# Letting the last 256 tokens enter a phase's first two GEMM tiles unnormed, in a hybrid attention and Mamba-2 backbone

## The chip, the cores and the metric

The kernel runs on one core of a Trainium2 chip. The metric is the device time of one execution in microseconds, the median of several runs. The engines are named as in the profile: PE is TensorE (PEld is its weight load), DVE VectorE, ACT ScalarE, POOL GpSimd, SP the engine that issues the DMAs.

## The reference, cut to what matters

Two layers over 512 latent tokens and a prefix of 256 context tokens, with 1024 features. Layer 0 mixes tokens with grouped-query attention, layer 1 with a bidirectional Mamba-2 state-space mixer (SSD), and a gated convolutional FFN of width 2816 follows each. Every sub-layer starts with an RMS norm and a modulation by a shift and a scale:

```python
def rms_norm(x, g):
    xf = x.astype(jnp.float32)
    y = xf * lax.rsqrt(jnp.mean(xf * xf, axis=-1, keepdims=True) + EPS)
    return (y * g.astype(jnp.float32)).astype(x.dtype)

def modulate(x, shift, scale):
    return x * (1 + scale) + shift
...
```

So the input of a sub-layer's first GEMM is, for feature d and token t, x[d, t] · gain[d] · rs[t] + shift[d], with gain = g · (1 + scale) and rs[t] the reciprocal root of the token's mean square. A GEMM with weights W gives for token t the product rs[t] · (W (x · gain)) + W shift: the factor rs and the term W shift can be put in behind the product.

## The kernel before, in words

Features lie on the 128 partitions and tokens in the free dimension, so the 1024 features are eight row tiles (KT = 8, index m where they are made, k where they are read). Every GEMM of width 1024 is done in three matmuls for one weight block and one row tile (`mm3`, L105, L106, L108): both factors are split into a high and a low half of a shorter format (`wh`, `wl`; `hh`, `hl`), and the products high·high, high·low and low·high are summed in PSUM. `load_w` (L85, L87) makes the two halves of a weight block: ScalarE casts the high one, VectorE subtracts for the low one.

A phase ends with `down` (attention output, FFN down product) or with the SSD's output product. They add their products to the residual rows `X`, one row tile m after the other, with a VectorE instruction per tile (L897 in `down`). They go over the tokens in segments (`ending`): first the 256 context tokens, then latent tokens 0 to 255, then latent tokens 256 to 511. As the rows of a segment are added, ScalarE squares them and they are summed (`Norm.sq`, L356 to L363; GpSimd adds most of them). When all eight are in, `rstd_rows` makes rs: two small matmuls over the partitions (`ss`, L267), a few small steps on VectorE and ScalarE (`rsa`, `rsy`, `rsu`, `rb`, L270 to L278), a transposition on TensorE (`rsT`, L284), and a copy by ScalarE (`rs`, L376). Then `modulated` makes each of the eight input rows of the segment: VectorE multiplies x · gain · rs (`ht`, L312). In even rows ScalarE adds the shift and writes the high half (L321), and VectorE makes the low half (L322); in odd rows ScalarE adds the shift (L317), casts the high half (L318), and GpSimd makes the low half (L319).

`first_tiles` holds the first two GEMM tiles of the next phase (`ps_first`, two PSUM tiles of 1024 columns, tag S). Their products run first for the segments that have their norm already and at the end for the last 256 latent tokens, while the norm of those goes on in the generator `bg`. There are three such boundaries. The first is from the attention's output product to FFN 0 (first products from 413 us on), the second from FFN 0 to the SSD (from 974 us on), the third from the SSD's output product to FFN 1 (from 1534 us on; no context tokens there). At the second, the two first tiles are `ps_dt`, the step sizes of the state space, and the first x tile. ScalarE reads `ps_dt` (`dte`, `dt`, L1031 and L1032), a chain of VectorE instructions follows (`dtu`, L1035 on, a reciprocal, four scans), and with its sums `acs` TensorE transposes (`ps_dtT`, L1252) and makes `ps_end` (L1258) from a VectorE copy of them (`acsT`, L1253). The convolution of x and B (`xf`, `Bf`, L1077) shares VectorE with that chain; `ps_xt` (L1121) and `ps_bt` (L1128) transpose x and B.

Each engine works through its own queue in a fixed order. A scheduler sets that order when the kernel is built, from the order of the program and from estimates of how long things take, so moving code also moves instructions on other engines.

## Time and profile before

| what | value |
|---|---|
| runs | 1911.81, 1906.7, 1911.2 us; median 1911.2 |
| the profiled execution, its time | 1909.82 us |
| the profiled execution, its span | 1908.0 us |
| granted TensorE clock, mean | 0.995 |
| busy share PE, DVE, ACT, POOL | 98%, 69%, 44%, 14% |
| chain that ended last: PE, DVE, issue, ACT | 79%, 9%, 4%, 2% |

The profile is of one execution. Its span runs from the first to the last instruction; the 1.8 us more of its time lie around it. A row of the timeline has start, duration, engine, line, operation, output and input, and the idle time before it with what released it. Matmuls overlap: one of 256 columns is listed with 0.28 us, while the next starts 0.12 us after it.

### The profile page before, as it was taken

What the parts mean: (1) busy time and instruction counts of PE and PEld (TensorE: products, weight loads), DVE (VectorE), ACT (ScalarE), POOL (GpSimd) and SP (SyncE); (2) the same over time, 40 slices, a digit from 0 to 9 for tenths busy, and PEclk for the clock granted to TensorE, in tenths of its full rate; (3) what the DMA queues carried; (4) which work ended last, traced back from release to release, by engine and by line L of the source; (5) the groups of instructions that cost most, each with busy time, mean ns of one, the idle gap of its engine ahead of it and who ended that gap; (6) DMA issues with size and microseconds to landing.
All of it is one profiled execution on the core that took longest, in us unless ns stands there. A gap on an engine that the chain in (4) does not pass through costs nothing.

```text
span 1908.0 us, 27239 instructions
## 1 busy us (share of the span) xinstructions
PE 1864.2 (98%) x10696; PEld 1527.1 (80%) x10696; DVE 1321.9 (69%) x1953; ACT 844.5 (44%) x1446; POOL 263.8 (14%) x246
## 2 busy tenths in 40 slices
PE   8899999989999999999989999999999999999999
PEld 6674546588888888888888888888888878888887
DVE  5578989678777777544488867777788466565555
ACT  3645644354122222222266677776666352323331
POOL 2200000031000000000040344344334210000000
PEclk8999999999999999999999999999999999999999
DMA  9123341014433555222223434434443223323232
GB/s 338 56 71 106 111 150 55 7 56 167 136 124 121 174 187 175 67 67 67 66 79 103 116 108 122 122 111 133 122 143 111 89 78 90 99 88 111 88 100 89
DMA packets 73424, 210.00 MB, mean 110 GB/s; under 512 B 8912, under 2 KB 14416, under 8 KB 73168
## 3 DMA queue, kind: packets, MB, share of 16 engines
q1 hardware_dynamic: 73296, 208.26, 35.0%
q8 instruction: 84, 1.38, 0.3%
q14 instruction: 44, 0.36, 0.1%
HBM read 198.79 MB, written 6.82 MB: 108 GB/s over the span
## 4 chain that ended last, share of the span: by engine, by line
PE 79%; DVE 9%; issue 4%; ACT 2%; POOL 1%; DMA 1%; SPq 0%; DVEq 0%; POOLq 0%; ACTq 0%
PE ps_up L106 10%; PE ps_up L108 10%; PE ps_up L105 10%; PE ps_d L105 6%; PE ps_d L108 6%; PE ps_d L106 6%; PE ps_in L108 4%; PE ps_in L106 4%; PE ps_in L105 4%; PE ps_o L687 2%; PE ps_s L723 2%; PE ps_st L1147 2%; DVE ht L312 1%; PE ps_wo L108 1%; PE ps_wo L105 1%
## 5 line engine op out<-in xcount | busy, mean ns | idle before, releaser
L87 DVE TENSOR_TENSOR wl<-wst,wh 128x1024 fp32r<-128x1024 f32 x209 | 260.4, 1246 | 243.3 <-PE ps_up L106 137.5
L85 ACT CAST wh<-wst 128x1024 fp32r<-128x1024 f32 x211 | 221.2, 1049 | 426.5 <-DMA wst<-in_wup 336.9
L106 PE MATMUL ps_up<-hlf,wh 128*128 128x512 f32 x1008 | 357.0, 354 | 0.0
L105 PE MATMUL ps_up<-hhf,wh 128*128 128x512 f32 x1008 | 356.9, 354 | 0.0
L108 PE MATMUL ps_up<-hhf,wl 128*128 128x512 f32 x1008 | 356.8, 354 | 0.0
L105 PEld LDWEIGHTS ps_up<-hhf,wh 128*128 128x128 f32 x1008 | 190.6, 189 | 26.5
L108 PEld LDWEIGHTS ps_up<-hhf,wl 128*128 128x128 f32 x1008 | 190.5, 189 | 26.4
L106 PEld LDWEIGHTS ps_up<-hlf,wh 128*128 128x128 f32 x1008 | 190.6, 189 | 26.2
L105 PE MATMUL ps_in<-hhs,wh 128*128 128x512 f32 (+1 forms) x560 | 204.4, 365 | 0.0
L106 PE MATMUL ps_in<-hls,wh 128*128 128x512 f32 (+1 forms) x560 | 199.4, 356 | 0.0
L108 PE MATMUL ps_in<-hhs,wl 128*128 128x512 f32 (+1 forms) x560 | 198.7, 355 | 0.0
L105 PE MATMUL ps_d<-hdh,wh 128*128 128x512 f32 (+1 forms) x568 | 193.6, 342 | 1.4 <-DVE X L897 1.2
L108 PE MATMUL ps_d<-hdh,wl 128*128 128x512 f32 (+1 forms) x568 | 193.5, 341 | 0.0
L106 PE MATMUL ps_d<-hdl,wh 128*128 128x512 f32 (+1 forms) x568 | 193.0, 340 | 0.3 <-DVE hdl L87 0.3
L897 DVE SCALAR_TENSOR_TENSOR X<-ps_d,mod,X 128x512 f32<-128x512 f32 (+1 forms) x224 | 124.9, 583 | 34.1 <-PE ps_d L108 33.6
L106 PEld LDWEIGHTS ps_d<-hdl,wh 128*128 128x128 f32 x568 | 106.6, 188 | 14.9 <-DVE hdl L87 0.7
L105 PEld LDWEIGHTS ps_d<-hdh,wh 128*128 128x128 f32 x568 | 106.3, 188 | 14.8 <-DVE X L897 1.4
L105 PEld LDWEIGHTS ps_in<-hhs,wh 128*128 128x128 f32 x560 | 105.9, 189 | 15.1 <-issue 1.0
L108 PEld LDWEIGHTS ps_in<-hhs,wl 128*128 128x128 f32 x560 | 105.8, 189 | 14.8
L108 PEld LDWEIGHTS ps_d<-hdh,wl 128*128 128x128 f32 x568 | 106.7, 188 | 13.1
L106 PEld LDWEIGHTS ps_in<-hls,wh 128*128 128x128 f32 x560 | 106.0, 189 | 13.2
L726 ACT ACTIVATE pr<-ps_s 128x1024 f32<-128x1024 f32 x56 | 57.1, 1020 | 97.5 <-PE ps_s L725 95.6
(341 smaller groups left out, 3493.7 us busy)
## 6 DMA issues: line engine op xcount, KB each, us to landing
wst<-in_wup SPq DMA_DIRECT2D x88, 512.0 KB, 3.6
wada<-in_adaT SPq DMA_DIRECT2D x56, 512.0 KB, 4.0
wst<-in_win SPq DMA_DIRECT2D x48, 512.0 KB, 3.7
wst<-in_wdown SPq DMA_DIRECT2D x44, 512.0 KB, 4.1
E<-ad SPq DMA_DIRECT2D x64, 256.0 KB, 6.8
wada<-in_adaB SPq DMA_DIRECT2D x24, 512.0 KB, 4.9
ec<-ead SPq DMA_DIRECT2D x64, 128.0 KB, 5.4
wst<-in_wout SPq DMA_DIRECT2D x16, 512.0 KB, 3.6
```

The source lines that it names most:

```text
L85: keep(nc.scalar.copy(hi, src))
L87: keep(eng.tensor_tensor(lo, src, _r(hi), ALU.subtract))
L105: mm(out, wh, ah, start=first, stop=False)
L106: mm(out, wh, al, start=False, stop=False)
L108: mm(out, wl, ah, start=False, stop=last)
L312: nc.vector.scalar_tensor_tensor(t[:, c0:c1], ap, g.moda[layer][ca][:, m, v : v + 1], rs[:, c0:c1], ALU.mult, ALU.mult)
L687: nc.tensor.matmul(po[S64[e], :n], v, pr[:, 512 * e + off : 512 * e + off + n], start=first, stop=last)
L723: nc.tensor.matmul(outs[e], a[S64[e], k], b[S64[e], q], start=i == 0, stop=False)
L726: nc.scalar.activation(pr, ps, AF.Exp)
L897: nc.vector.scalar_tensor_tensor(ap, o[:, c0:c1], gate[:, m, v : v + 1], ap, ALU.mult, ALU.add)
L1147: nc.tensor.matmul(ps[:, d * 256 : (d + 1) * 256], Bt[:, t * P : (t + 1) * P], xw[d][t], start=t == ts[0], stop=t == ts[-1])
```

## The change

The last segment (latent tokens 256 to 511, `LAST`) now enters the first two tiles as x · gain, without rs and without the shift. Each of its rows is made when it is added to `X` (`Norm.scaled`): ScalarE writes the high half (L373 of the new kernel), VectorE the low half (L374). The products of these rows come first, then those of the context, then those of latent tokens 0 to 255. The input of this last run has two more columns, which hold the shift (`Norm.bias`), so that W · shift falls out of the same matmuls in two PSUM columns. For them the input tiles got eight more floats in front: every input row now begins 32 bytes into its tile. Once rs of the last segment is there, three VectorE instructions per tile put it right in PSUM: a copy of two columns, the product with rs, the sum with W · shift (L472 to L474).

The rows that have their norm (`Norm.rows`) are made where `down` and `first_tiles` call for them: those of the context from the last `down` tiles on and between the products of the first run, those of tokens 0 to 255 between the products of the second, and those of the last segment, which the rest of the phase needs normed, in the third. All low halves of these rows are now VectorE's; GpSimd makes none of them. In the SSD the second x tile of the first group goes to two PSUM banks (`single`). At the third boundary the last tile of the output product is done in halves of its depth, alternating between the two column halves, and the weights of the first tiles are loaded ahead of it. The constant of ones is kept in the shorter format. The lines left out are the passing of the new objects from phase to phase.

```diff
+PAD = 8
+def wide(g, name):
+    return tuple(g.p.tile([P, PAD + L], F32R, tag=f"h{L}", bufs=16, name=f"{p}{name}") for p in ("hh", "hl"))
 def htiles(g, n, name):
+    if n == L:
+        return tuple(t[:, PAD:] for t in wide(g, name))
...
+    def scaled(self, x, m):
+        g, nc = self.g, self.g.nc
+        layer, ca, _ = self.a
+        t = self.tile(f"xa{self.name}")
+        hi, lo = t[:, : L // 2], t[:, L // 2 :]
+        gain = g.moda[layer][ca][:, m, 0:1]
+        (ap, _, _), = parts(x[0][m], *LAST[1:])
+        nc.scalar.activation(hi, ap, AF.Identity, scale=gain)
+        nc.vector.scalar_tensor_tensor(lo, ap, gain, _r(hi), ALU.mult, ALU.subtract)
+        self.early[m] = hi, lo
+    def bias(self, m):
+        g, nc = self.g, self.g.nc
+        layer, _, cb = self.a
+        b = g.mod[layer][cb][:, m, 0:1].broadcast_to([P, 2])
+        hi, lo = (t[:, PAD - 2 : PAD] for t in self.w[m])
+        nc.scalar.copy(hi, b)
+        nc.vector.tensor_tensor(lo, b, _r(hi), ALU.subtract)
...
         for m in range(KT):
-            modulated(g, self.h[i][m], x[i], rs, a, b, *self.a, self.streams[i][1], m, pool=m % 2)
+            if i == a == 0:
+                self.bias(m)
+            modulated(self.g, self.h[i][m], x[i], self.rs[seg], a, b, *self.a, self.streams[i][1], m)
             yield
...
-def first_tiles(g, ws, norm, bg):
-    ends = ending(norm.streams)
-    for _ in gemm_in(g, tiles, norm.h, (0, L), [ends[:-1], ends[-1:]]):
-        next(bg, None)
-    for _ in bg:
+def first_tiles(g, ws, norm, x):
+    nc = g.nc
+    half = L // 2
     tiles = [(S(g, "ps_first"), w) for w in ws]
+    chain = norm.chain(LAST)
+    runs = [(2 * half, lambda k: norm.early[k]), (half - 2, lambda k: tuple(t[:, PAD - 2 : PAD + half] for t in norm.w[k]))]
+    if len(norm.streams) > 1:
+        runs.insert(1, (3 * half, lambda k: norm.h[1][k]))
+    todo = norm.todo + [None]
+    for i, (c0, h) in enumerate(runs):
+        if i == len(runs) - 1:
+            for _ in chain:
+                pass
+            todo[i] = norm.rows(LAST, x)
+        n = 0
+        for ps, w in tiles:
+            for k in range(KT):
+                ks = slice(k * P, (k + 1) * P)
+                o = ps[:, c0 : c0 + h(k)[0].shape[-1]]
+                mm3(g, (w[0][:, ks], w[1][:, ks]), [(o, h(k))], k == 0, k == KT - 1)
+                next(chain, None)
+                if n % 2:
+                    next(todo[i], None)
+                n += 1
...
+    for ps, _ in tiles:
+        v, b = ps[:, 2 * half : 3 * half], g.p.tile([P, 2], F32, tag="rst", bufs=8, name="wb")
+        nc.vector.tensor_copy(b, ps[:, half - 2 : half])
+        nc.vector.tensor_tensor(v, v, norm.rs[LAST], ALU.mult)
+        nc.vector.tensor_scalar(v, v, b[:, 0:1], None, ALU.add)
...
@@ down
                 if norm:
                     norm.sq((i, a, b), x, m)
+                    if (i, a, b) == LAST:
+                        norm.scaled(x, m)
             next(bg, None)
+            if norm and gi == 1 and m > 4:
+                next(todo[0])
...
@@ ssd
-            ps = ps_x0 if gi == j == 0 else gemm(ld(j), (1, 0))
+            ps = (ps_x0[:, :L], ps_x0[:, L:T]) if gi == j == 0 else gemm(ld(j), (1, 0), gi == 0)
...
+    half = [Bank(g, "ps_wo")[:, : L // 2] for _ in SEGS[0]]
+    for ks in (range(8), range(8, 16)):
+        for (_, a, b), ps in zip(SEGS[0], half):
+            m_tile(m, ws, ps, a, b, ks, bg)
+            if ks[0]:
+                add_out(m, ps, a, b)
+                nxt.sq((0, a, b), [xn], m)
+                if a:
+                    nxt.scaled([xn], m)
+                else:
+                    bg = nxt.chain((0, a, b), 1)
...
```

The order of the instructions is best seen at three places. The first is TensorE's queue near the end of the attention's output product, where the first products of FFN 0 come in (`ps_d` is a tile of the output product, `hhol` and `hlol` the attention's result, `hhf_0` and `hlf_0` normed rows). Before:

```order
L267 MATMUL ssf_3975<-ones,sqf_3890 128x1 x2
L105 MATMUL ps_first<-hhf_0_3612,wh 128x256
L106 MATMUL ps_first<-hlf_0_3613,wh 128x256
L105 MATMUL ps_first<-hhf_0_3612,wh 128x256
L106 MATMUL ps_first<-hlf_0_3613,wh 128x256
L105 MATMUL ps_d_3988<-hhol_3220,wh 128x256
L106 MATMUL ps_d_3988<-hlol_3221,wh 128x256
```

And after (`xaf` is a scaled row):

```order
L108 MATMUL ps_d_3990<-hhol_3588,wl 128x256
L105 MATMUL ps_first<-xaf_3923,wh 128x256
L106 MATMUL ps_first<-xaf_3923,wh 128x256
L108 MATMUL ps_first<-xaf_3923,wl 128x256
L105 MATMUL ps_first<-xaf_3940,wh 128x256
L106 MATMUL ps_first<-xaf_3940,wh 128x256
L108 MATMUL ps_first<-xaf_3940,wl 128x256
L105 MATMUL ps_first<-xaf_3957,wh 128x256
L106 MATMUL ps_first<-xaf_3957,wh 128x256
L108 MATMUL ps_first<-xaf_3957,wl 128x256
L284 MATMUL rsTf_4008<-cst,rbf_3971 128x128 x2
L105 MATMUL ps_d_4012<-hhol_3220,wh 128x256
```

Four products of a normed row stood between the tiles of the output product before; now eleven products of scaled rows stand there (two of a second weight block, which repeat a row above, are in the queue as well), and all of the other scaled products follow the last `ps_d`.

The second place is VectorE's queue at the second boundary, from the last normed rows to the chain through `dtu` (`hls` low halves, `hhs` high halves, `rss` the norm's factor, `wb` the two columns of W · shift). Before:

```order
L322 SCALAR_TENSOR_TENSOR hls_4_4313<-ht,mod_92,hhs_4_4312 128x256
L87 TENSOR_TENSOR wl<-wst,wh 128x1024
L322 SCALAR_TENSOR_TENSOR hls_6_4317<-ht,mod_92,hhs_6_4316 128x256
L1063 MEMSET raw_9259 128x2 x3
L1063 MEMSET raw_9260 128x2
L1025 TENSOR_SCALAR na<-na 128x1
L1063 MEMSET raw_9260 128x2 x2
L1035 TENSOR_SCALAR dtu<-dte 128x384
```

And after:

```order
L332 SCALAR_TENSOR_TENSOR hls_5_4351<-ht,mod_94,hhs_5_4350 128x256
L322 SCALAR_TENSOR_TENSOR ht<-X,moda_102,rss 128x256 x2
L472 COPY wb<-ps_first 128x2 x2
L332 SCALAR_TENSOR_TENSOR hls_6_4353<-ht,mod_94,hhs_6_4352 128x256
L332 SCALAR_TENSOR_TENSOR hls_7_4355<-ht,mod_94,hhs_7_4354 128x256
L473 TENSOR_TENSOR ps_first<-ps_first,rss 128x256 x2
L474 TENSOR_SCALAR ps_first<-ps_first,wb 128x256 x2
L1109 TENSOR_SCALAR na<-na 128x1
L1147 MEMSET raw_9331 128x2 x3
L1147 MEMSET raw_9332 128x2 x3
L87 TENSOR_TENSOR wl<-wst,wh 128x1024
L1119 TENSOR_SCALAR dtu<-dte 128x384
```

The correction of the two tiles (L473, L474) now stands behind all rows of the last segment and ahead of `dtu`, and a weight split moved from the rows to a place just ahead of `dtu`.

The third place is TensorE's queue at the end of the C tile of the SSD's first group (`ps_in` with `hhs_7` is its last product, `ps_in` with `hhs_0` the first of the z tile). Before:

```order
L1252 MATMUL ps_dtT<-cst,dt 128x128 x3
L105 MATMUL ps_in<-hhs_0_4304,wh 128x512
L106 MATMUL ps_in<-hls_0_4305,wh 128x512
L108 MATMUL ps_in<-hhs_0_4304,wl 128x512
L105 MATMUL ps_in<-hhs_1_4306,wh 128x512
L106 MATMUL ps_in<-hls_1_4307,wh 128x512
L1258 MATMUL ps_end<-acsT,cst 128x192 x2
L1121 MATMUL ps_xt<-cst,xf 128x128 x8
L108 MATMUL ps_in<-hhs_1_4306,wl 128x512
L1121 MATMUL ps_xt<-cst,xf 128x128 x4
```

And after:

```order
L108 MATMUL ps_in<-hhs_7_4354,wl 128x512
L1336 MATMUL ps_dtT<-cst,acs 128x128 x3
L1336 MATMUL ps_dtT<-cst,dt 128x128 x3
L1342 MATMUL ps_end<-acsT,cst 128x192 x2
L1205 MATMUL ps_xt<-cst,xf 128x128 x12
L105 MATMUL ps_in<-hhs_0_4340,wh 128x512
L106 MATMUL ps_in<-hls_0_4341,wh 128x512
L108 MATMUL ps_in<-hhs_0_4340,wl 128x512
```

Five products of the z tile that stood ahead of `ps_end`, and a sixth that stood among the `ps_xt`, now stand behind all of them.

More of the change, by code (lines that the diff above doesn't have):

```diff
@@ L460, in attention @@
     for _ in range(24):
-        nc.tensor.matmul(warm[:, :P], g.ones, g.ones, start=True, stop=True)
+        nc.tensor.matmul(warm[:, :P], g.warm, g.warm, start=True, stop=True)
     acc = t3(g, "acc", n=L)
@@ L625, in q_units @@
             nc.scalar.copy(qs[:, c0 : c0 + n], ps[:, :n])
-    onesr = g.const.tile([P, P], F32R, name="onesr")
-    nc.scalar.copy(onesr, g.ones)
+    onesr = g.onesr
     id2 = g.const.tile([P, HD], F32, name="id2")
@@ L885, in down @@
     bg = iter(())
-    for group in order:
+    todo = []
+    for gi, group in enumerate(order):
         for m in ms:
@@ L904, in down @@
                 pass
-            bg = norm.gen(group[0], x, 2)
-    return bg
+            if group[0] != LAST:
+                bg = norm.chain(group[0])
+                todo.append(norm.rows(group[0], x))
+    if norm:
+        norm.todo = todo
 def ffn(g, layer, streams, x, h, first, nxt=None, side=iter(()), after=()):
@@ L989, in ffn, with ssd @@
         ln_exp(g)
-    return flush(pend, [[s] for s in ending(streams)], nxt, after), wf
-def ssd(g, x, norm, wf, bg, close):
+    flush(pend, [[s] for s in ending(streams)], nxt, after)
+    return wf
+def ssd(g, x, norm, wf, close):
     nc, I, tc = g.nc, g.I, g.tc
@@ L998, in ssd @@
     h = norm.h
-    ps_dt, ps_x0 = first_tiles(g, wf, norm, bg)
+    ps_dt, ps_x0 = first_tiles(g, wf, norm, x)
     ph = ExitStack()
@@ L1013, in ssd, with gemm @@
     tok = lambda t: slice(t * P + (2 if t >= 4 else 0), (t + 1) * P + (2 if t >= 4 else 0))
-    def gemm(w, streams):
+    def gemm(w, streams, single=False):
+        if single:
+            ps = [Bank(g, "ps_in1") for _ in range(2)]
+            for i in streams:
+                for _ in gemm_in(g, [(ps[i], w)], h, (0, 0), [[(i, 0, (L, C)[i])]]):
+                    pass
+            return ps[0], ps[1]
         ps = S(g, "ps_in")
@@ L1017, in gemm @@
             pass
-        return ps
+        return ps[:, :L], ps[:, L:T]
     H2 = 64
@@ L1417, in body @@
     wf = firsts(g, I["wup"][0, 0], I["wup"][0, NFT])
-    bg = down(g, ws, [g.oT[f] for f in (5, 6, 7)], g.mod[0][2], streams, x, [[s] for s in ending(streams)], nrm)
-    first = first_tiles(g, wf, nrm, bg)
+    down(g, ws, [g.oT[f] for f in (5, 6, 7)], g.mod[0][2], streams, x, [[s] for s in ending(streams)], nrm)
+    first = first_tiles(g, wf, nrm, x)
     pha.close()
```

78 lines of the change are left out of this document (45 added, 33 removed).

## The prediction

> **What bounds the kernel now.** The page comes first: TensorE is busy nearly all the time, so the end moves only where TensorE stands still or where it gets other work to do.
>
> ```profile
> span 1908.0 us, 27239 instructions
> PE 1864.2 (98%) x10696; PEld 1527.1 (80%) x10696; DVE 1321.9 (69%) x1953; ACT 844.5 (44%) x1446; POOL 263.8 (14%) x246
> ```
>
> TensorE's work is not changed by more than a few columns, so I read the three places the diff touches, first by equal windows (columns: length, then busy time and count of each engine, granted clock, DMA).
>
> ```profile
> 393.00:413.00 20.00, 19.42 (x157) 18.81 (x157) 15.76 (x34) 11.88 (x29) 10.08 (x12) 1.00 0.09 28
> 413.00:433.00 20.00, 16.57 (x128) 15.37 (x128) 17.37 (x37) 12.17 (x33) 9.13 (x11) 1.00 0.25 79
> 433.00:453.00 20.00, 18.74 (x126) 16.99 (x126) 14.51 (x23) 13.62 (x22) 4.21 (x4) 1.00 0.40 159
> 973.90:993.90 20.00, 16.41 (x127) 15.19 (x128) 17.39 (x37) 12.27 (x33) 9.12 (x11) 1.00 0.56 185
> 1525.00:1545.00 20.00, 17.36 (x119) 15.56 (x117) 13.71 (x31) 9.27 (x23) 3.79 (x4) 0.91 0.18 54
> ```
>
> In the 20 us ahead of the first boundary (attention to FFN) 0.6 us is idle, at it 3.4 and then 1.3. The second (FFN to SSD, 973.9) has the same shape. The third (SSD to FFN) loses 2.6 in its first 20 us, and only there the granted clock falls, to 0.91. VectorE is at 87% at the first two: it is the next engine to watch. The waits of TensorE between 404 and 446 say who was late:
>
> ```profile
> PE ps_first L106 <- POOL hlf L319: 1.5, 3, 0.7
> PE rsTf L284 <- DVE rbf L278: 1.2, 2, 1.0
> PE ps_d L105 <- DVE X L897: 1.1, 1, 1.1
> PE ps_first L105 <- ACT hhf L318: 0.5, 1, 0.5
> PE ps_first L106 <- DVE hlf L322: 0.5, 1, 0.5
> ```
>
> Nine stalls, 4.8 us (columns: total, times, longest). Behind a stall the next matmul starts 0.22 and not 0.12 us later (1537.05, 1537.27 below), so each loses 0.1 more: 5.7 us.
>
> At the third boundary the stalls are only part of it:
>
> ```profile
> 1533.87 0.50 PE L105 MATMUL ps_first<-hhf,wh 128*128 128x256 f32 x2 [0.64 <-ACT hhf L321]
> 1537.05 0.39 PE L106 MATMUL ps_first<-hlf,wh 128*128 128x256 f32 x1 [1.04 <-POOL hlf L319]
> 1537.27 0.31 PE L108 MATMUL ps_first<-hhf,wl 128*128 128x256 f32 x1
> 1538.45 0.41 PE L108 MATMUL ps_first<-hhf,wl 128*128 128x256 f32 x1
> 1538.66 0.41 PE L105 MATMUL ps_first<-hhf,wh 128*128 128x256 f32 x1
> 1553.94 0.28 PE L106 MATMUL ps_first<-hlf,wh 128*128 128x256 f32 x1
> 1554.06 0.28 PE L108 MATMUL ps_first<-hhf,wl 128*128 128x256 f32 x1
> ```
> ```profile
> 1534.00:1537.00 3.00, 1.61 (x8) 1.00 (x8) 3.00 (x6) 2.57 (x6) 1.46 (x2) 1.00 0.58 178
> 1537.00:1540.00 3.00, 2.95 (x15) 2.95 (x16) 3.00 (x8) 1.82 (x4) 0.87 (x1) 0.57 0.00 0
> 1540.00:1543.00 3.00, 3.00 (x24) 2.98 (x23) 1.84 (x6) 2.24 (x7) 1.26 (x2) 0.87 0.01 3
> ```
>
> The 96 first products last from 1533.87 to 1554.18, 20.3 us. At 0.12 each they need 11.5, with three early 512-column matmuls, a sum and a transpose 12.8: 7.5 us lost, and 0.64 ahead of them, 8.1. Inside it lie some 3 us at a granted clock of 0.57, where matmuls start 0.21 instead of 0.12 us apart: 14 matmuls by 0.09, 1.3 us. That stretch follows three microseconds in which TensorE was busy 1.61.
>
> The Trainium skill, TensorE: Matmul & The Clock Gate, Part 1, has the array at half rate after an idle window of about 3.4 us, until it has been busy as long. The trace agrees on the depth and the length; but here sparse work was enough, no wait was longer than 1.04 us. Dense products should end this stretch; I count it inside the 8.1.
>
> **The change part by part.** *First boundary.* When the last `down` tile ends, the 48 products of the unnormed last 256 tokens need only scaled rows, and most of those rows exist: 48 × 0.12 = 5.8 us of work wait for TensorE where before it had four products and then stalled on `X`, `rbf` and `hhf`. What may run late is VectorE. All low halves are now its own (12 move from GpSimd), and it makes 8 more for the scaled rows. Prices:
>
> ```profile
> 993.93 2.07 DVE L312 SCALAR_TENSOR_TENSOR ht<-X,moda,rss 128x256 f32<-128x256 f32 x5 [1.03 <-ACT rss L376]
> 981.77 1.04 DVE L312 SCALAR_TENSOR_TENSOR ht<-X,moda,rss 128x256 f32<-128x256 f32 x1
> L312 DVE SCALAR_TENSOR_TENSOR ht<-X,moda,rss 128x256 f32<-128x256 f32 x19 | 11.1, 618 | 2.0 <-ACT rss L376 2.0
> 986.32 0.42 DVE L361 TENSOR_TENSOR sqs<-sqs 128x256 f32<-128x256 f32 x1
> 983.13 1.21 DVE L87 TENSOR_TENSOR wl<-wst,wh 128x1024 fp32r<-128x1024 f32 x1
> 1034.03 0.29 DVE L1279 TENSOR_SCALAR nacs<-acsT 128x256 f32<-128x256 f32 x1
> ```
>
> Five 256-column steps back to back take 2.07, 0.40 each; a lone one took 1.04 while GpSimd made a low half beside it, and the mean of the nineteen `ht` at the second boundary is 0.62. With GpSimd gone from here I take 0.40 (bounds 0.40 and 0.62): its rows are the ones with nothing beside them. Behind the last `X` update stand 20 `ht` and 20 low halves, 16 us, and 3.8 of other things (one weight split 1.2, the statistics, squares, one scaled row), then the correction in PSUM (two by 0.42, two by 0.29, small copies: 1.6). Up to the last normed row that the first tiles read, the queue is 24 × 0.40 + 3.8 = 13.4 us; TensorE's own work over that stretch is 133 × 0.12 = 16.0. So it fits, by a little: I leave 1.0 us for stalls, where a low half waits for ScalarE's high half and the queue runs dry for a moment. The eight pairs of the last 256 tokens then run beside the next tile, at 0.80 a pair against three 512-column matmuls (0.23 each, below) or 0.69: another 0.9. The correction ends some 8 us after the products; FFN tile 0's convolution reads it, and TensorE has two more tiles before that is wanted. Gain 5.7 − 1.9 = **3.8** (0 if every step stays at 0.62, 5.7 if no stall is left). The two extra columns are 1/128 of 48 products, 0.05 us; the 16 two-column bias steps (8 on ScalarE, 8 on VectorE) and the earlier weight loads come while the last `down` or output tiles run, where both engines wait for TensorE. The 32-byte start I take at nothing; no row of before has a shifted read, so its price is a rival.
>
> *Second boundary.* At the end of the first tiles TensorE is 5.7 − 1.0 = 4.7 ahead. But here their reader is a chain:
>
> ```profile
> 1002.64 0.58 ACT L1031 ACTIVATE dte<-ps_first,par 64x384 f32<-64x384 f32 x1 [0.42 <-PE ps_first L108]
> 1005.32 0.36 DVE L1035 TENSOR_SCALAR dtu<-dte 128x384 f32<-128x384 f32 x1 [2.90 <-ACT dte L1033]
> 1027.25 2.08 DVE L1077 SCALAR_TENSOR_TENSOR Bf<-raw,par,Bf 128x770 f32<-128x770 f32 x2
> 1029.25 0.55 DVE L1253 COPY acsT<-ps_dtT 128x384 f32<-128x384 f32 x1
> 985.14 0.47 DVE L897 SCALAR_TENSOR_TENSOR X<-ps_d,mod,X 128x256 f32<-128x256 f32 x1
> 1027.02 0.49 PE L1252 MATMUL ps_dtT<-cst,acs 128*128 128x128 f32 x3
> 1027.59 0.48 PE L105 MATMUL ps_in<-hhs,wh 128*128 128x512 f32 x1
> 1029.85 0.92 PE L1258 MATMUL ps_end<-acsT,cst 128*128 128x192 f32 x4 [0.87 <-DVE acsT L1253]
> 1036.51 0.82 PE L1128 MATMUL ps_bt<-cst,Bf 128*128 128x128 f32 x6
> ```
> ```profile
> 1013.90:1045.00 31.10, 30.22 (x159) 25.48 (x159) 28.14 (x37) 21.15 (x37) 0.00 (x0) 1.00 0.37 105
> ```
>
> Before, ScalarE read `ps_first` at 1002.64, 2.7 us ahead of `dtu`. Now it must wait for the correction, the end of VectorE's 21.4 us: the last `X` update (985.14) comes some 1.6 earlier, the wait on `X` and half a microsecond of the transposes' waits being gone, so 983.5 + 0.4 + 21.4 = 1005.3, and `dtu` starts at 1008.0, 2.7 later than before. VectorE is busy 28.1 of the 31 us from 1013.9 on, so it stays late. TensorE, 4.7 ahead, reaches `ps_dtT` and `ps_end` at about 1022.3 (1027.02 − 4.7), and the new order puts `ps_end` and all of `ps_xt` ahead of the z product, which stood there as filler. `acsT` now follows the x taps directly (two B taps less ahead of it, 2.0) and one weight split less (1.2): 1029.25 + 2.7 − 3.2, about 1028.8. So TensorE idles six microseconds and is where it was, owing the five z products (1.2 us) that it had done. `ps_bt` waits for a B that is later too. I put the net loss at 1.0, between a gain of 4.7, if the chain were on time, and a loss of 5, if all 2.7 of it and the wait for B come on top.
>
> At the third boundary three sparse microseconds were followed by a stretch at 0.57 that cost 1.3; six idle ones make the same likely here. Part of that lies under the wait for B, so I add 0.5 of the 1.3: **+1.5**. By the rule of the clock gate page named above the half rate would be sure here, since the gap is longer than its window; taken in full, the second boundary would be +2.3 and the forecast 0.8 later.
>
> *Third boundary.* The output product's last tile now ends both column halves within 24 matmuls (2.8 us), so the first half's norm starts later, but 48 unnormed products (5.8) cover it. Left over: waits at the two transposes (0.9), rows behind the second norm's `rbf` on VectorE (1.0), 16 pairs at 0.80 against 0.72 and 0.69 (1.5): 3.4. Of 8.1 that frees **4.7** (1, if VectorE's steps keep 0.62 in 16 pairs, to 7, if only the transposes wait).
>
> Sum: −3.8 + 1.5 − 4.7 = −7.0. The profiled execution took 1909.82, 1.4 below the median 1911.2 of the runs; from the median the forecast is **1904**.
>
> **The rivals.** *(a) The second boundary keeps its gain too*: the chain through `dtu` isn't late, because the scheduler's order still lets the correction in early. Then −3.8 − 4.7 − 4.7 = −13.2, 1898. For: the windows are twins. Against: the `dtu` chain ended in a wait at `ps_end` already (0.87). *(b) The second boundary eats the others*: `dtu`'s 2.7 us come through to the end of the z products in full, and the half rate with them (2.7 + 1.3, and 1.0 for B): +5.0, so −3.8 − 4.7 + 5.0 = −3.5, 1908, which is no change. For: VectorE full behind `dtu`. Against: before, TensorE waited only 0.9 us there. *(c) Slower, VectorE paces all three*: the steps stay near 0.55 although GpSimd is gone, since each low half waits for a ScalarE row. That is 40 × 0.15 = 6.0 at each of the first two and 32 × 0.15 = 4.8 at the third, 16.8 in all, +9.8 beside the −7.0: 1921. It turns to slower from 7.0 / 112 = 0.06 more a step on, at 0.46. Against: runs of five at 0.40. *(d) The 32-byte start slows every 512-column read*: half a per cent of 1864 us is +9, with the −7.0 1913; a full per cent would make it slower. No row speaks for it.
>
> **How the numbers follow.** Forecast 0.52 (own range 1899 to 1909), (a) 0.14, (b) 0.19, (c) 0.11, (d) 0.04: VectorE's runs of five make (c) the unlikely end, and (a) needs a chain that isn't late although its input is. A measurement of this kernel tells about 0.3%, 5.7 us, from no change: faster is below 1905.5. The forecast's case lies there with 0.36 of its 0.52, (a) with all, (b) with 0.02: 0.52. Slower (above 1916.9) is (c) and half of (d): 0.13. The rest, 0.35, is the same. The range leaves out the ends of (a) and (c): 1896 to 1914.
>
> **What would show it.** Right: the waits on `hlf`, `X` and `rbf` are gone at 404 to 446, and the next FFN starts some 4 us earlier; the third boundary's clock stays at 1.00; at the second, one wait of about six microseconds at `ps_end`, then half the clock, with `dtu` 2 to 3 us late against the end of the first tiles. Wrong: first products waiting for low halves from VectorE at each row (c), `ht` still above 0.5, or no wait at `ps_end` (a); matmul spacing of 512 columns above 0.227 in the rows below would be (d).
>
> ```profile
> 1036.05 0.39 PE L106 MATMUL ps_in<-hls,wh 128*128 128x512 f32 x1
> 1036.28 0.40 PE L108 MATMUL ps_in<-hhs,wl 128*128 128x512 f32 x1
> ```

## The result and the profile after

The changed kernel takes 1922.45 us (median of 6 runs, 1920.11 to 1925.05); before took 1908.55 beside it (6 runs, 1906.16 to 1911.81). The ratio is 1.0072 [1.0057, 1.0087]: 13.9 us slower, where 7 us less were forecast, and outside the range.

The page of after, its first lines:

```profile
span 1918.3 us, 27309 instructions
PE 1875.1 (98%) x10696; PEld 1527.1 (80%) x10696; DVE 1350.8 (70%) x2051; ACT 845.3 (44%) x1463; POOL 232.2 (12%) x214
```

TensorE has the same 10696 matmuls and was as busy by share, but its busy time grew by 10.9 us. Little of the loss is idle time; most of it is matmuls that take longer. The windows of after, at the places shown of before:

```profile
393.00:413.00 20.00, 19.76 (x165) 19.29 (x164) 15.60 (x38) 12.15 (x32) 10.17 (x13) 1.00 0.04 13
413.00:433.00 20.00, 19.03 (x154) 18.46 (x153) 18.36 (x46) 12.01 (x30) 1.56 (x3) 1.00 0.15 53
433.00:453.00 20.00, 19.00 (x114) 16.67 (x112) 16.79 (x36) 11.28 (x17) 0.00 (x0) 1.00 0.42 159
453.00:473.00 20.00, 15.97 (x70) 13.14 (x71) 17.63 (x29) 7.07 (x9) 0.00 (x0) 0.83 0.63 210
973.90:993.90 20.00, 19.16 (x155) 18.31 (x154) 17.89 (x42) 11.53 (x29) 4.17 (x5) 1.00 0.57 185
1525.00:1545.00 20.00, 19.99 (x136) 18.16 (x134) 13.16 (x27) 9.00 (x21) 3.47 (x4) 1.00 0.43 131
```

The boundaries themselves did what they were to do: TensorE is busy 19.0 us where it was 16.6 (413), 19.2 where it was 16.4 (973.9), 20.0 where it was 17.4 (1525), and there the clock stays at 1.00. But 20 us behind the first boundary, at 453, stands a hole that before did not have, with the clock at 0.83. The waits of TensorE in after, in order of the windows 404 to 446, 446 to 500, 965 to 1060 and 1525 to 1565:

```profile
PE rsTf L284 <- DVE rbf L278: 0.5, 1, 0.5
PE ps_first L106 <- DVE hlf L332: 0.4, 1, 0.4
...
PE ps_up L108 <- DVE wl L87: 3.9, 1, 3.9
PE ps_up L105 <- ACT wh L85: 1.1, 1, 1.1
...
PE ps_end L1342 <- DVE acsT L1337: 5.8, 1, 5.8
PE rsTs L284 <- DVE rbs L278: 1.0, 2, 0.8
PE ps_in L105 <- ACT dt L1116: 0.6, 1, 0.6
...
PE ps_first L105 <- ACT hhf L331: 0.9, 1, 0.9
```

Eight stalls of 4.8 us at the first boundary became two of 0.9 (the prediction speaks of nine; the five rows that it shows add up to eight). In their place stand 5.0 us a little later, on the weights of FFN 0, and 5.8 at `ps_end`. The rest is seen in the groups of the matmuls (busy time, then the mean ns of one). Before:

```profile
L105 PE MATMUL ps_up<-hhf,wh 128*128 128x512 f32 x1008 | 356.9, 354 | 0.0
L105 PE MATMUL ps_in<-hhs,wh 128*128 128x512 f32 (+1 forms) x560 | 204.4, 365 | 0.0
L105 PE MATMUL ps_d<-hdh,wh 128*128 128x512 f32 (+1 forms) x568 | 193.6, 342 | 1.4 <-DVE X L897 1.2
```

After:

```profile
L105 PE MATMUL ps_up<-hhf,wh 128*128 128x512 f32 x1008 | 360.3, 358 | 1.1 <-ACT wh L85 1.1
L105 PE MATMUL ps_in<-hhs,wh 128*128 128x512 f32 (+1 forms) x560 | 206.0, 368 | 0.6 <-ACT dt L1116 0.6
L105 PE MATMUL ps_d<-hdh,wh 128*128 128x512 f32 (+1 forms) x568 | 193.5, 342 | 0.2
```

`ps_up` and `ps_in` read the input tiles that now begin 32 bytes in, and are 4 and 3 ns longer. `ps_d` reads tiles that were not shifted, and is the same. How far apart the matmuls start is read from one `up` tile in the middle of FFN 0, by the start of its first 512-column matmul and that of the 256-column one behind its 24th. Before, (640.48 − 635.01) / 24 = 0.228:

```profile
635.01 0.40 PE L105 MATMUL ps_up<-hhf,wh 128*128 128x512 f32 x1
...
640.48 0.28 PE L105 MATMUL ps_up<-hhf,wh 128*128 128x256 f32 x1
```

After, (640.76 − 635.22) / 24 = 0.231:

```profile
635.22 0.40 PE L105 MATMUL ps_up<-hhf,wh 128*128 128x512 f32 x1
...
640.76 0.28 PE L105 MATMUL ps_up<-hhf,wh 128*128 128x256 f32 x1
```

Over the tiles of this kind 24 starts take 5468 ns before and 5540 after for `ps_up` in FFN 0, 5453 and 5561 (means) in FFN 1, and 5474 and 5572 for `ps_in`; the context's 256-column matmuls, whose tiles were not shifted, are 0.120 apart in both. With 42 latent tiles in the `up` of each FFN and 47 in the SSD that is 42 × 0.072 + 42 × 0.108 + 47 × 0.098 = 12.2 us, if none of it falls where TensorE waits anyway.

Following one matmul after the other through both traces gives the whole account of after against before: the change's own effect is +14.0 us between the start of the first boundary and the end (in the attention, which it does not touch, this execution was 3.7 us quicker; the executions of the kernels below differ there by −6.2 to +1.4). Of it 3.2 arise from the first boundary to 518 us, 2.5 in the rest of FFN 0, 10.0 from the second boundary to the SSD's output (its last `ps_y`, at 1457 us in before), −5.5 from there through the third boundary, 3.9 in FFN 1.

### The profile page after: what moved, and what is told of

Its sections match the earlier page's. It is cut to its first block, busy times and chain, and to the rows that moved or that the text cites. A ratio compares the mean times of both kernels' runs of the same rounds, so it can differ in the third digit from the quotient of the medians.

```text
span 1918.3 us, 27309 instructions
## 1 busy us (share of the span) xinstructions
PE 1875.1 (98%) x10696; PEld 1527.1 (80%) x10696; DVE 1350.8 (70%) x2051; ACT 845.3 (44%) x1463; POOL 232.2 (12%) x214
## 4 chain that ended last, share of the span: by engine, by line
PE 77%; DVE 11%; ACT 3%; issue 3%; DMA 1%; POOL 0%; SPq 0%; DVEq 0%; ACTq 0%; POOLq 0%
PE ps_up L106 10%; PE ps_up L105 10%; PE ps_up L108 10%; PE ps_d L105 6%; PE ps_d L108 6%; PE ps_d L106 6%; PE ps_in L106 4%; PE ps_in L108 4%; PE ps_in L105 4%; PE ps_s L792 2%; PE ps_o L756 2%; PE ps_st L1231 2%; DVE xf L1161 2%; DVE wl L87 1%; PE ps_wo L106 1%
## 5 line engine op out<-in xcount | busy, mean ns | idle before, releaser
L106 PE MATMUL ps_up<-hlf,wh 128*128 128x512 f32 (+1 forms) x1008 | 360.2, 358 | 0.0
L106 PEld LDWEIGHTS ps_in<-hls,wh 128*128 128x128 f32 x560 | 106.1, 189 | 14.5
```

What stands on the lines that cost most here:

```text
L106: mm(out, wh, al, start=False, stop=False)
```

## The experiments

The kernels with another start, and all that are built on them, keep four instead of six of a kind of buffer in the attention, to make room. Each time stands beside runs of before on the same chip. Before's own median was between 1908.3 and 1913.8 in these sessions, so kernels of different sessions are compared by their ratios and by the traces. Where a loss or gain "by the traces" is given, it is the difference to before in the start of the same matmul at two places.

**The 32 bytes alone, in before.** Before, with its latent input tiles eight floats in and nothing else.

```diff
+PAD = 8
 def htiles(g, n, name):
+    if n == L:
+        return tuple(g.p.tile([P, PAD + L], F32R, ...)[:, PAD:] for p in ("hh", "hl"))
```

> This is the kernel before with one thing of the change alone: the 512-column input tiles begin 32 bytes in (eight floats in front); nothing else of it. To make room, the attention phase has four instead of six buffers of 512 floats. Theory A, the shifted start slows every 512-column read of these tiles: the start-to-start time of 512-column matmuls from the input tiles goes from 227 to about 231.5 ns (24 matmuls of a tile 5.54 instead of 5.47 us), the tiles of context columns (256, unshifted) stay at 120, and the time goes up by 8 to 14 us over the kernel before. Rival B, the slower matmuls come from something else of the change (its order, VectorE's traffic): 227 ns and within 2 us of the kernel before.

Measured: 1921.72 against 1913.76, ratio 1.0047 [1.0033, 1.0061], 9.0 us. An `up` tile of FFN 0 takes 5540 ns and one of the SSD 5571, as in after. Outside the boundaries its trace loses 2.9 us in FFN 0, 3.0 in the SSD and 4.4 in FFN 1: 10.3 in all. In the SSD that is less than the tiles add up to (4.6), in the FFNs it is about the same. So the start costs about 10 us, with nothing else of the change in the kernel.

**After with other starts: 256, 64 and 128 bytes.**

```diff
-PAD = 8
+PAD = 64    # then 16, then 32
```

> The changed kernel with 64 floats in front instead of 8: all input rows begin at a multiple of 256 bytes (again four instead of six small buffers in the attention phase). Theory A: 512-column matmuls at 227 ns again, the time falls by 9 to 12 us against the changed kernel's 1922 and stands 2 to 5 us above the kernel before; what is left over is the wait at ps_end (5 to 6 us), the wait for a weight's low half in FFN 0 (about 4 us) and the half clock behind both. Rival B: 231 ns as in the changed kernel, 1920 to 1925. Rival C, the change is as the prediction put it but for the shift: the time would then be 1904 or less, 5 us or more below the kernel before.

> The changed kernel with 16 floats in front: rows begin at multiples of 64 bytes, 2112 bytes apart. If 64 bytes are the grain, 227 ns; if the grain is 256 bytes, the matmuls of a tile differ among themselves again with a pattern over the row tiles and the mean stays near 230 to 232.

> The changed kernel with 32 floats in front: rows begin at multiples of 128 bytes, 2176 bytes apart. Grain of 64 or 128 bytes: 227 ns. Grain of 256 bytes: two kinds of row tile in turn, mean 229 to 232.

Measured: 256 bytes 1913.35, ratio 1.0001 [0.9991, 1.0011], with 5468 and 5474 ns per tile, before's values. 64 bytes: 1922.03 (one run), 5566 and 5554 ns. 128 bytes: 1923.63 (one run), 5502 and 5548. In FFN 1 the medians are 5440 for 256 bytes, as in before, 5547 for 64, 5600 for 128 and 5560 in after. So 256 bytes take the price away and the steps below don't. In after each tile is 2080 bytes long and the starts drift by 32 bytes from one tile to the next; the spacing repeats every four row tiles, eight buffers, 256 bytes. The starts fit a grain of 256 bytes, where 32, 64 and 128 inside it all cost. Why it is so is not shown, and the length of a tile was changed together with its start each time.

But without the shift the change still gains nothing: the 7 us that were forecast beside it are missing. By the trace the version with 256 bytes loses 3.1 us from the first boundary to 518 us, 7.3 from the second to the SSD's output, and gains 6.2 at the third.

**Only the third boundary.** The version with 256 bytes, with before's code (`old_down`, `old_first_tiles`, `OldNorm`) for the first two boundaries.

```diff
-    first = first_tiles(g, wf, nrm, x)
+    first = old_first_tiles(g, wf, nrm, bg)
@@ ssd
-    ps_dt, ps_x0 = first_tiles(g, wf, norm, x)
+    ps_dt, ps_x0 = old_first_tiles(g, wf, norm, bg)
```

> Rows begin at multiples of 256 bytes, and only the third boundary (SSD to FFN 1) is as changed; the first and the second are as before. Theory A (the third gains 6 us, as the milestones of the two traces show, and the other two give nothing or lose): 5 to 7 us below the kernel before, ratio about 0.997. Rival, the third boundary's gain is only the half-clock stretch that happened to fall into the profile of before: 0 to 2 us.

Measured: 1910.59 against 1912.9, ratio 0.999 [0.9977, 1.0003]. By the trace the third boundary gained 6.5 us, and 2.4 at the first and 5.7 from the second to the SSD's output were lost again, although these run before's code. The low halves of odd rows (count, then ns of the shortest, the median and the longest) and the wait at the first boundary:

```profile
L329 POOL TENSOR_TENSOR hlf<-ht,hhf x12: 726/882/3664, 410.1 to 441.1; 128x256 fp32r<-128x256 f32 x12
L329 POOL TENSOR_TENSOR hls<-ht,hhs x12: 730/824/3668, 973.4 to 1005.9; 128x256 fp32r<-128x256 f32 x12
```
```profile
PE ps_first L106 <- POOL hlf L329: 3.5, 3, 2.8
```

One GpSimd instruction of 3.66 us stands at each. The first lasts from 435.87 to 439.53, while VectorE goes through five row steps, 0.40 apart without a gap, and a weight split that ends at 438.96. Before's longest took 1.60. So before's own boundaries vary by several us between executions; the profile of the first experiment has the same two waits of 2.8, and those of before and of the versions below with one of before's boundaries have none.

**FFN 0's next weights first.** At 453 the weights are late, and the trace says why. SP's DMA queue in after, in order:

```profile
441.11 0.33 SPq L157 DMA_DIRECT2D cb<-in_cflat  x1
441.48 1.58 SPq L164 DMA_DIRECT2D wada<-in_adaT  x3
443.17 0.40 SPq L95 DMA_DIRECT2D wst<-in_wup  x1
452.60 3.93 SPq L164 DMA_DIRECT2D wada<-in_adaT  x2
```

and the wait of its first row:

```profile
SPq L157 <- DVE ps_first L473: 23.5, 1, 23.5
```

`cb`, an operand of side work for the next layer, goes to memory that the attention leaves; it waits for the last reader there, now the correction in PSUM, and a block of `wup` stands behind it. In before it waits for a low half and starts at 441.07. In after TensorE ends the first tiles 8.7 us earlier (3.7 of them from ahead of the boundary), and this queue goes on no earlier. In this kernel the next four weight blocks of FFN 0 are loaded ahead of `cb`, which is ordered behind them.

```diff
...
+    after(nc.sync.dma_start(cb, g.I["cflat"].broadcast_to([P, 2 * D])))
...
+    pre = {t: load_w(g, I["wup"][layer, t]) for t in ((1, NFT + 1, 2, NFT + 2) if nxt else ())}
...
-            w = load_w(g, I["wup"][layer, t])
+            w = pre.pop(t, None) or load_w(g, I["wup"][layer, t])
```

> The changed kernel with rows at multiples of 256 bytes (e2), and in FFN 0 the weights of the next four tiles are loaded ahead of the side work's load of the conditioning vector (1 MB) and its first three weight rows, which wait in the same DMA queue for the PSUM correction. Theory A (SP's queue stood still behind that load until the correction at 442.7, so that the weights of the fourth tile came late): the waits of 1.6 and 3.9 us at 453 to 459 and the half clock behind them go, 5 to 7 us below e2. Rival, VectorE is what made the weight's low half late (its queue full of correction, convolution and side work): the wait stays at 2 us or more, within 2 us of e2.

Measured: 1908.81 against 1912.9, ratio 0.9975 [0.9964, 0.9986], 4.8 us below before, and 5.0 below the version without the edit by the ratios. The window that was at 15.97 and a clock of 0.83, and the wait in it:

```profile
453.00:473.00 20.00, 20.00 (x123) 17.98 (x122) 17.79 (x31) 9.21 (x10) 0.00 (x0) 1.00 0.40 134
```
```profile
PE ps_up L108 <- DVE wl L87: 0.2, 1, 0.2
```

The first boundary now gives 2.5 us up to 518.

**Is that edit a gain by itself?** The same edit in before.

> The kernel before with the loads of FFN 0's next four weight blocks ahead of the side work's loads, the edit of e6 alone. Theory A (before, TensorE came to the fourth tile 1.6 us after its weights were ready): within 1 us of the kernel before. If it is 3 us or more below it, e6's gain was the edit's own and has nothing to do with the change.

Measured: 1910.91 against 1909.24, ratio 1.0005 [0.9994, 1.0016]. Before's weights came in time, so nothing. The edit repairs what the change brought.

**The z product ahead of `ps_end`.** In the version with 256 bytes, and then together with the early weights, z is written ahead of the transposes, to give TensorE before's filler back.

```diff
-            if gi == 0 and i == 3:
+            if gi == 0 and i == 4:
...
```

> e2, and in the SSD's first group the z product is written ahead of the transposes that wait for the scans, so that TensorE has the z tiles to do while VectorE finishes. Theory A (the second boundary loses what TensorE idles at ps_end and the half clock behind it): the 6.0 us wait at ps_end falls under 1 us and the time by 4 to 7 us against e2. Rival, VectorE's chain through dtu sets the end of this stage whatever TensorE does: the wait only moves behind the z tiles (to ps_xt, ps_bt or ps_st), within 2 us of e2.

> e2 with the edits of e6 and e7. If both theories hold, the gains add: 10 to 13 us below e2 and so below the kernel before, about 1900 against its 1910. If both rivals hold, as e2.

Measured: 1914.99, ratio 1.0007 [0.9997, 1.0017]; with the weights 1909.0, ratio 0.9975 [0.9964, 0.9986]. Neither differs from its version without it. The edit did not reach its aim: the scheduler left z behind `ps_end`, and the wait there grew to 7.1 us, with a weight split on VectorE just ahead of `acsT` (1032.32 and 1033.45). So neither theory was tried.

**Odd low halves back on GpSimd.** In the version with the early weights, at all three boundaries.

```diff
-            modulated(self.g, self.h[i][m], x[i], ..., self.streams[i][1], m)
+            modulated(self.g, self.h[i][m], x[i], ..., self.streams[i][1], m, pool=m % 2)
```

> e6 with one part of the change undone: the low halves of odd rows are GpSimd's again at all three boundaries (ScalarE casts for them once more). Theory A (VectorE's load, not the waiting of TensorE, sets the second boundary, and the 12 low halves moved to it are half of what it got more): dtu starts 2 to 4 us earlier against the end of the first tiles, and the time falls 1 to 4 us below e6. Rival, GpSimd's low halves cost VectorE as much as they take from it (ht at 0.62 us instead of 0.40 beside them) and stall TensorE's first products at the end: same as e6 or slower by up to 5 us.

Measured: 1914.35 against 1909.24, ratio 1.0031 [1.0021, 1.004]: slower. By the traces it gains 0.2 us at the first boundary, loses 9.6 from the second to the SSD's output and gains 4.6 at the third, where the version with the early weights gains 2.5, loses 7.3 and gains 6.2. The two groups at the first boundary, here:

```profile
L327 DVE SCALAR_TENSOR_TENSOR ht<-X,moda,rsf 128x256 f32<-128x256 f32 x24 | 12.9, 578 | 0.0
L337 DVE SCALAR_TENSOR_TENSOR hlf<-ht,mod,hhf 128x256 fp32r<-128x256 f32 x12 | 8.0, 674 | 0.3 <-ACT hhf L336 0.2
```

and with all low halves on VectorE:

```profile
L337 DVE SCALAR_TENSOR_TENSOR hlf<-ht,mod,hhf 128x256 fp32r<-128x256 f32 x24 | 10.7, 487 | 0.2 <-ACT hhf L336 0.2
L327 DVE SCALAR_TENSOR_TENSOR ht<-X,moda,rsf 128x256 f32<-128x256 f32 x24 | 10.5, 480 | 0.0
```

VectorE does the 36 steps in 20.9 us beside GpSimd, and all 48 in 21.2 alone. Here GpSimd takes work over and gives VectorE nothing back.

**First and third boundary only.** The version with the early weights, with before's second boundary.

```diff
-    nxt = Norm(g, 1, 1, 0, streams, "s")
+    nxt = OldNorm(g, 1, 1, 0, streams, "s")
...
-    ps_dt, ps_x0 = first_tiles(g, wf, norm, x)
+    ps_dt, ps_x0 = old_first_tiles(g, wf, norm, bg)
```

> e6 with the second boundary (FFN 0 to SSD) as before, the first and the third as changed. Theory A (the second boundary loses about 4 us net, 3.9 by the milestones of e2's trace): 3 to 5 us below e6, ratio to the kernel before about 0.995. Rival, what e2 loses there it would lose later in the SSD anyway: same as e6.

Measured: **1900.01** against 1909.24 (1897.92 to 1902.16), ratio **0.9954 [0.994, 0.9968]**, the quickest of all with the whole computation. By the trace it gains 2.9 at the first boundary, 6.6 at the third, and between the second boundary and the SSD's output it is before's equal to 0.1. So the new second boundary costs what the version with the early weights loses there, 7.3 us.

**The correction ahead of the last rows, at the second boundary.**

```diff
-            todo[i] = norm.rows(LAST, x)
+            todo[i] = norm.rows(LAST, x) if norm.name != "s" else None
...
```

> e6, and at the second boundary the correction in PSUM stands ahead of the last segment's eight rows and not behind them. If the length of the chain (correction, dte, dtu) is what counts: the ScalarE part of it runs beside the rows, dtu 3 to 4 us earlier, 3 to 4 us below e6. If VectorE's total work counts: only its 1.2 us of idle time ahead of dtu goes, 0 to 1.5 us below e6.

Measured: 1910.98 against 1909.24, ratio 1.0008 [0.9998, 1.0018], and 8.9 us lost there by the trace instead of 7.3; no gain. VectorE's rows say that the edit worked and what it ran into:

```profile
999.31 0.49 DVE L479 TENSOR_SCALAR ps_first<-ps_first,wb 128x256 f32<-128x256 f32 x1
...
1008.53 0.36 DVE L1126 TENSOR_SCALAR dtu<-dte 128x384 f32<-128x384 f32 x1 [2.36 <-ACT dte L1124]
```

The correction ends 5.3 us earlier than without the edit (999.80 against 1005.14), but `dtu` begins at 1008.53, not earlier than there (1007.56): ScalarE makes `dte` only behind the high halves of the last rows, which now end at 1004.30, and behind a small instruction (`na`) that starts at 1005.76. So the correction alone is not what holds `dtu`. What an earlier `dtu` would be worth was not seen, since none came.

**How much of the second boundary is VectorE?** Two kernels leave the eight VectorE instructions of the x convolution of the first group out (7.5 us, so the output isn't the reference's): one with the new second boundary, one with the old. A third leaves nothing out, and sets the copy of the sums (`acsT`) ahead of those eight.

```diff
-        for tap in (0, 1, 3, 4):
+        for tap in (0, 1, 3, 4) if j > 1 else ():
...
```

> The version with the early weights, but the eight VectorE instructions of the convolution of the first group's two x tiles (7.5 us) are left out, so the output isn't the reference's. Theory V (VectorE is the bound from the last normed rows to the copy of the sums): the wait of 6.0 us at the ends of the sums goes to under 1.5, the half clock behind it goes too, and the stretch from the second boundary to the last output product, 488.7 us with the taps, falls to 482 to 484; 5 to 7 us less in all. Rival F (TensorE's own order, with the z products behind the ends of the sums, is what costs): the wait goes but the stretch stays at 486 or more, since TensorE then has to wait for the next thing.

> The version with only the first and third boundary changed, with the same eight instructions left out. Theory V: before's order waits only 0.9 us for VectorE there, so at most 1.5 us less than with the taps (481.9 us for the stretch), and the two versions without taps are within 3 us of each other. Rival F: this one stays 4 us or more ahead of the other.

> The version with the early weights, with nothing left out, but the copy of the transposed sums on VectorE stands ahead of the eight taps of x. Theory V: VectorE's work is the same, so the wait only moves, from the ends of the sums to the transposes of x behind them, 6 to 7 us; the time is within 2 us of the version with the early weights. Rival F: the ends of the sums come 5 us earlier and the chain behind them too; 3 us or more are gained.

Measured: 1902.27 against 1908.28 for the first, ratio 0.9966 [0.9954, 0.9979]. The wait at `ps_end` is gone, and from the second boundary to the SSD's output it loses 1.3 us to before instead of 7.3. The second took 1915.75, ratio 1.0039 [1.0026, 1.0053], with less work than the quickest kernel; its waits between 1060 and 1470 show a new one:

```profile
PE ps_xt L1293 <- DVE ec L1386: 11.8, 7, 2.4
```

Without the eight instructions the scheduler set another order for the later groups, and the transposes there wait. So its time says nothing on the question. Its first group, ahead of those waits, does: at the matmul that before starts at 1060 us it has gained 1.2 us on before since the second boundary began, and the first kernel 2.8, within the 3 us that theory V allows. The third took 1907.1, ratio 0.9994 [0.9984, 1.0005], with 6.0 lost there by the trace, and the wait has only moved, as theory V has it:

```profile
1019.80 0.92 PE L1355 MATMUL ps_end<-acsT,cst 128*128 128x192 f32 x4 [0.32 <-DVE acsT L1347]
1027.65 3.12 PE L1215 MATMUL ps_xt<-cst,xf 128*128 128x128 f32 x12 [6.94 <-ACT xf L1175]
```

In the output product the third kernel then loses 3.0 more, where the version with the early weights loses 0.9, so the new order gains nothing. In the first group it is VectorE's amount of work that is late, not its order: with 7.5 us less of it the 7.3 us lost fall by 6.0.

The same traces show that this is only a part of the loss. From the second boundary to the matmul at 1060 us the version with the early weights loses 3.2 us; from there to the SSD's output, in the later groups, it loses 4.1. Without the eight instructions the first part is a gain of 2.8, and the second is a loss of 4.1 again. Every kernel with the new second boundary and all its work written in that order (after, 256 bytes, early weights, z first, GpSimd, correction first), and the first kernel here too, has one and the same order of TensorE's later groups, another than before's. Those of them without the 32-byte start lose 3.7 to 4.3 us there, with these waits among them:

```profile
PE ps_xt L1212 <- DVE ec L1305: 1.3, 1, 1.3
PE ps_y L1312 <- ACT E L1275: 1.3, 1, 1.3
PE ps_cb L1257 <- ACT Cf L1172: 0.6, 1, 0.6
```

The quickest kernel has before's order there and loses nothing. The third kernel here has before's order but for three of 2370 matmuls, and loses 0.5. So more than half of the 7.3 us goes with an order that the scheduler set anew for later groups, which the change does not touch. No run puts before's order there and leaves the rest of the new boundary alone.

## Why the prediction was wrong, point by point

**The 32-byte start, "I take at nothing".** This failed, and it is the largest term: 9.0 us [6, 12] in before alone, 10.3 by that kernel's trace. It was rival (d), with a chance of 0.04 and the words "no row speaks for it"; its price, 9, and its sign in the spacing were right, as was the row named to show it. It was half a per cent. "No row" was lack of evidence on either side: before had no read that began anywhere else.

**First boundary, −3.8.** Up to the end of the first tiles the working held: stalls of 0.9 instead of the 1.0 left over, VectorE's steps 0.40 apart, TensorE 4.9 us ahead (4.7 were forecast). The step that failed is "TensorE has two more tiles before that is wanted". It asked only for the correction. The weights behind `cb` in SP's queue were wanted too, and came when they had always come; 5 us of wait followed, and in after half the clock:

```profile
455.00:458.00 3.00, 0.24 (x1) 0.25 (x2) 3.00 (x6) 0.00 (x0) 0.00 (x0) 0.61 0.39 89
458.00:461.00 3.00, 3.00 (x8) 2.32 (x9) 3.00 (x7) 0.85 (x1) 0.00 (x0) 0.50 0.78 309
461.00:464.00 3.00, 3.00 (x12) 2.40 (x11) 2.92 (x5) 1.78 (x2) 0.00 (x0) 0.75 0.60 193
```

The Trainium skill, TensorE: Matmul & The Clock Gate, Part 1, has this after an idle window of about 3.4 us. The trace agrees on the half rate; but the gap of 3.9 us began at 453.9, and the clock fell about 1.8 us into it (0.61 over 455 to 458 is 1.00 for 0.7 us and 0.50 for 2.3), with two matmuls, 0.73 us of work, in the 3.4 us ahead of the fall. Net +3.1 instead of −3.8; with the weights first, −2.5 to −2.9 in the seven traces in which VectorE makes all low halves. Of what is still missing of the 4.9, 0.9 is waited for at 495 to 498 (0.6 for the cast of a `down` weight, 0.3 for `X`), in the version with the weights first; the rest has no wait that names its cause.

**Second boundary, +1.5.** Each event that was forecast came; the price was mis-sized, and the sum stopped too early. In after:

```profile
1007.81 0.87 DVE L474 TENSOR_SCALAR ps_first<-ps_first,wb 128x256 f32<-128x256 f32 x2
...
1011.11 0.36 DVE L1119 TENSOR_SCALAR dtu<-dte 128x384 f32<-128x384 f32 x1 [1.17 <-ACT dte L1117]
...
1030.68 0.55 DVE L1337 COPY acsT<-ps_dtT 128x384 f32<-128x384 f32 x1
```

This execution was 2.0 us behind before as the boundary began, so `dtu` is 3.8 later than before (2.7 forecast), `acsT` 0.6 earlier (0.4), the wait 5.8 (six). TensorE was then to be "where it was" and to lose 1.5. In the traces without the shift it lost 7.3. The version with the early weights shows the parts: it is 0.5 ahead at `ps_end`, then owes six z products (1.4), runs some 3 us at a clock of 0.50 and some at 0.80, waits 0.6 for B, and in the later groups waits 2.1 us more than before (5.2 against 3.1), in an order of the groups that the scheduler set anew; some 2 us are not assigned. By the same matmuls the first group costs 3.2 us, where 1.5 was forecast, and the later groups 4.1, for which the prediction has no term. So the step that failed is that TensorE, once it is "where it was" and owes the z products, has nothing more to lose: it followed the new order of the queue to the end of the first group and took the groups behind it as before's. Rival (b), a loss of 5.0 at 0.19, was nearer.

**Third boundary, −4.7.** Right in mechanism, and more: −6.2 with 256 bytes and with the weights first, −6.5 alone, −6.6 in the quickest version. The clock stays at 1.00 in after where it fell to 0.57:

```profile
1534.00:1537.00 3.00, 3.00 (x28) 3.00 (x27) 2.28 (x4) 0.97 (x3) 0.00 (x0) 1.00 0.11 16
1537.00:1540.00 3.00, 3.00 (x28) 3.00 (x27) 2.08 (x9) 2.76 (x11) 0.00 (x0) 1.00 0.44 161
```

Of the 3.4 us counted as left over, half was hidden. **Rival (c)** was wrong: nothing paces the rows at 0.55; the mean of `ht` fell from 0.61 to 0.48.

The sum with the measured terms: 3.1 + 7.3 − 6.2 + 10.3 = +14.5, against 14.0 by the trace and 13.9 by the times. One thing does not close. The versions with 256 bytes and with the early weights come out at +4.1 and −1.4 by the traces, but at +0.2 and −4.8 by their ratios, while the kernels that ran beside a before of 1908 to 1909 agree within 1.5 us (the quickest: −9.4 and −8.8), but for the old second boundary without the eight instructions (+2.9 and +7.4). The versions with 256 bytes and with the early weights ran where before's median was 1913, and both kernels with before's boundaries that were profiled there had the GpSimd instruction of 3.66 us. That before had it too would explain the gap; no profile of before was taken there, so this stays argued. If it is so, the 4.8 us that the early weights stand below before are rather 1.4.

## What to carry to other kernels

When a change moves where tiles begin, price the start of every later read of them, not only the few columns it adds: 1 to 2% of a 512-column matmul, in 3100 of them, outweighed the 6 us that the change gained at its best boundary. When an engine is brought forward by 5 us, look 20 us on for what it will want next, in the DMA queue above all, and for what its queue's head waits for: a transfer that nobody needs soon can hold the one that is needed. And filling an engine's idle time in front of a stretch that another engine bounds can only move the wait into that stretch. Where a scheduler sets the queues, compare their order far behind the change too: 4.1 of the 7.3 us went with it. Here the change is worth taking at two of the three boundaries, with 256 bytes and the weights first, and then it gains 0.46%.

## What the runs showed of the hardware that was not expected

- 512-column matmuls in the 4-byte format (fp32r) start 0.229 to 0.233 us apart (medians over a tile) where their moving tiles begin 32, 64 or 128 bytes in and are 2080, 2112 or 2176 bytes long, and 0.227 to 0.228 where they begin 256 bytes in and are 2304 long, or are as in before.
- A GpSimd instruction of 0.73 us took 3.66 while VectorE ran a series of instructions without a gap. The Trainium skill, SBUF — State Buffer, SBUF: two separate sides, says that, where VectorE reads two inputs from SBUF and GpSimd reads SBUF too, the one that starts first holds their shared port pair for its whole instruction and the other blocks. VectorE's instructions here have two such inputs (`ht` from `X` and `rsf`). The trace agrees with this as the cause, which no run isolates; the blocked one then lost to six instructions in a row.
- Sparse work is enough for the lower clock: behind the 2.8 us wait of the third-boundary-only kernel, with TensorE busy 1.8 and 1.4 us in the two stretches of 3 us ahead, the granted clock was 0.53 for 3 us.
